# A macaron decoder layer on one core: paired units in a written order on VectorE and ScalarE, splits emitted a step ahead, gating weight tile by weight tile

## The chip, the cores and the metric

The kernel runs on one core of a Trainium2 chip. The metric is the device time of one execution in microseconds, the median of several runs. A core has a matrix engine (TensorE, PE in the profile), whose weight loads are shown as PEld, and VectorE (DVE), ScalarE (ACT), GpSimd (POOL) and SyncE (SP). Each executes its own list of instructions in order; semaphores tie the lists together. SP issues the DMA transfers here.

## The reference

One layer of a decoder, for 1024 tokens of width 1024 in float32:

```
x = x + 1/2 * SwiGLU_1(RMSNorm(x))            # d_ff = 2816
z = RMSNorm(x) @ w_in                          # [u | v | c_q | c_kv | k_rope | q_mem | gates A, B, C]
u, v = gelu(z_u), gelu(z_v)
y_a = u * (tril(W_s) @ layernorm(v) + b_s)     # spatial gating, chunks of 128 tokens, 8 groups of 64
y_b = latent attention(c_q, c_kv, k_rope)      # 8 heads, rotary, q and k normalized, causal
y_c = attention(q_mem, mem)                    # 4 heads, 256 memory tokens
x = x + (sum_i sigmoid(gate_i + b_gate) * (y_i @ W_branch_i)) @ w_out
x = x + 1/2 * SwiGLU_2(RMSNorm(x))
```

`SwiGLU(h)` is `(silu(h @ W_g) * (h @ W_u)) @ W_down`.

## The kernel before

**Precision.** Every float32 operand of a large matrix product is split: ACT rounds it to a high part (`split`, a cast or copy), DVE subtracts the high part from it for the low part. `mm3` then runs three matmuls: high by high, high by low, low by high. So each weight and each activation tile costs a pass of ACT, then one of DVE, before PE can use it: PE's second and third matmul of a group wait for the low parts.

**Seven products.** The feed-forward blocks and the gates are computed in blocks of two by two with seven products instead of eight (`Seven`). Activations have the operands b11, b12, b21, b22 and the sums t1 to t4; weights have a11, a12, a21, a22 and the sums s1 to s4. `OpNorm` makes the activation operands: `norm(half, p)` normalizes a tile, `put` splits it; t1, t2 and t4 come by one DVE addition or subtraction for each tile, in place, and t3 with b22 from the first half alone. `Seven.sums(f)` makes a unit's four weight sums on DVE, `Seven.weights(f, part)` splits the parts "a", "s", "t" and "l" of them. `product` is one call of 12 matmuls; a unit `f` of two output tiles takes seven such calls.

**The order of a block.** While the second half of the tokens is still being normalized, only t3 and b22 are ready. `units` therefore runs two units at once (f and g): first `s3*t3` and `s4*b22` for both; in between, `norm.sums(1)` (token sums of squares on PE, then an inverse square root on DVE) and `norm.turn(1)` (the scale turned by PE transposes into a PSUM bank); then, as b11, b21, t2, t1 and t4 appear, a11, a12, s2, s1 and a22 for both. After each output `emit` adds the pieces and applies the function (silu and product for a feed-forward block, sigmoid for a gate). `units` is called in three places: in `SwiGLU.start` for units 1 and 2 of FFN1, in `Gates.run` for gate units 0 and 1, and in `Kernel.run` for units 0 and 1 of FFN2. The remaining units go one by one through `unit` (`up`, `Gates.run`).

**Down.** `SwiGLU.down` is the second phase, again with seven products: seven loops, each over 11 tiles of the inner dimension in six steps of two (the last of one). A step fetches ahead, splits its weight tiles and its operand (`wide` gives the room: two tags of 5 buffers each), runs 24 matmuls into four banks, does the in-place sums that later loops need (`then`) and a few `acts` (accumulations of an earlier loop's banks into x, and the next norm's work). `next(aside)` advances a generator: `late_constants` loads 14 small constants and then makes rotary tables on DVE in pieces.

**Spatial gating.** `sgu` runs v and then u through `gelu_rows`, two tiles of 128 tokens at a time: `zrow` runs all eight weight tiles for one token tile, then for the next. v is normalized on DVE, split, and used as the operand of the gating products; u is multiplied by them.

**What sets the order.** Dependencies and semaphores come from the framework, and so does the order of each engine's list: a planner with a time model takes what is ready, the first emitted first. Inside `manual_schedule(engines=...)` the named engines keep the order of emission. In `start` these are PE, DVE, ACT and SP; in the other two calls of `units`, in `up` and the gates PE alone; in `down` PE and SP. Spatial gating is left to the planner.

In `units` the part after the first four calls reads, before:

```python
norm.b11(0)
if not early:
    w[f] |= self.weights(f, "a")
norm.b11(1)
for u in fs:
    ...
    self.product(a[u], w[u], "a11", "b11")
    p1[u] = k.row()
    nc.scalar.copy(p1[u], a[u])
    norm.b21(0 if u == f else 1)
```

Of the kernel before, what the change touches and what calls it, by code (L numbers as in the profile page):

```python
# [40 lines left out]
class Kernel:  # L41
# [506 lines left out]
    def gelu_rows(self, dst, h, i, w, pair):  # L548

        gelu = lambda d, x: self.nc.scalar.activation(d, x, ACT.Gelu)  # L550
        ps = self.mm() if pair else None
        for k in range(2):
            b = ps[:, k] if pair else self.bank()
            self.zrow(b, h, i + k, w)
            if not pair:
                gelu(dst[:, k], b)
        if pair:
            gelu(dst, ps)

    def sgu(self, h):  # L560
        nc, a, tc = self.nc, self.a, self.tc
        with tc.tile_pool(name="sgu", bufs=1) as p:
# [12 lines left out]
            for hf in range(2):  # L575
                vhi, vlo = (p.tile([P, 4, SGW], F32R, name=n, bufs=2) for n in ("v_hi", "v_lo"))
                vs.append((vhi, vlo))
                for i in range(0, 4, 2):
                    st = self.small.tile([P, 2, 6], F32, name="bn", tag="bn")
                    mv = self.small.tile([P, 2, 2], F32, name="mv", tag="mv")  # L580
                    v = self.raw().rearrange("p (k d) -> p k d", k=2)
                    self.gelu_rows(v, h, hf * 4 + i, w, i == 2)
                    for k in range(2):
                        nc.vector.bn_stats(st[:, k], v[:, k])
                        nc.vector.bn_aggr(mv[:, k], st[:, k])
                    r = self.rms(mv[:, :, 1], 2, 1)
                    for k in range(2):
                        nc.vector.scalar_tensor_tensor(
                            v[:, k], in0=v[:, k], scalar=mv[:, k, 0:1], in1=ln_g, op0=ALU.subtract, op1=ALU.mult)
                        nc.vector.scalar_tensor_tensor(  # L590
                            v[:, k], in0=v[:, k], scalar=r[:, k:k + 1], in1=ln_b, op0=ALU.mult, op1=ALU.add)
                    self.split(vhi[:, i:i + 2], vlo[:, i:i + 2], v)
            w = self.load(a["w_u"])
            yt = [self.split_pair() for _ in range(4)]
            for hf in range(2):
                u, v = p.tile([P, 4, SGW], F32, name="u"), vs[hf]
                for i in range(0, 4, 2):
                    self.gelu_rows(u[:, i:i + 2], h, hf * 4 + i, w, i == 0)
# [387 lines left out]
    def run(self):  # L986
# [12 lines left out]
        with tc.tile_pool(name="f1", bufs=1) as fp, self.banks("f1ps") as self.pm:  # L999
# [6 lines left out]
                lambda: nc.sync.dma_start(g_ffn1, a["ffn1_norm"]))  # L1006
            ffn.up(3)
# [7 lines left out]
            def sink(half, c):  # L1015
# [5 lines left out]
                [*first, *gates.first()], self.late_constants())  # L1021
# [4 lines left out]
        with tc.tile_pool(name="f2", bufs=1) as fp, self.banks("f2ps") as self.pm:  # L1026
# [9 lines left out]
            with tc.manual_schedule(engines={mybir.EngineType.PE}):  # L1036
                ffn.units((0, 1), early=True)
# [22 lines left out]
class OpNorm:  # L1060
# [22 lines left out]
    def norm(self, half, p, after=None):  # L1083


        t, s, v = self.t.t[half, p], self.s[half], self.k.nc.vector
        if self.scaled:
            i = v.tensor_tensor(t, t, s.unsqueeze(1).to_broadcast([P, 2, 512]), op=ALU.mult)
            if after is not None:
                self.k.after(i, after)  # L1090
            return t
        for k in range(2):
            c = 2 * p + k
            i = v.scalar_tensor_tensor(
                t[:, k], in0=t[:, k], scalar=self.gain()[:, c:c + 1], in1=s, op0=ALU.mult, op1=ALU.mult)
            if after is not None:
                self.k.after(i, after)
        return t

    def put(self, name, p, src, room=None):  # L1100
# [3 lines left out]
        self.mark = k.split(hi, lo, src)  # L1104
# [13 lines left out]
    def b11(self, p):  # L1118
        self.put("b11", p, self.norm(1, p))

    def b21(self, p):
        self.put("b21", p, self.norm(1, 2 + p, self.mark))

    def t2(self, p, room):

        t = self.t.t[1, p]
        self.k.nc.vector.tensor_tensor(t, self.t.t[0, p], t, op=ALU.add)
        self.put("t2", p, t, room)

    def t1(self, p, room):  # L1130
# [3 lines left out]
        self.put("t1", p, t, room)  # L1134

    def t4(self, p, room):
# [3 lines left out]
        self.put("t4", p, t, room)  # L1140


class Seven:
# [87 lines left out]
    def units(self, fs, w=(), late=0, turn=2, early=False, asides=()):  # L1231
# [11 lines left out]
        if early:  # L1243
            for f in fs:
                w[f] |= self.weights(f, "a")
# [15 lines left out]

        aside()
        norm.b11(0)
        if not early:
            w[f] |= self.weights(f, "a")
        norm.b11(1)
        for u in fs:
            a[u] = k.single()
            if u == g and not early:
                w[u] |= self.weights(u, "a")  # L1270
            self.product(a[u], w[u], "a11", "b11")
            p1[u] = k.row()
            nc.scalar.copy(p1[u], a[u])
            norm.b21(0 if u == f else 1)
# [3 lines left out]
        w[f] |= self.weights(f, "s")  # L1278
        for p in range(2):
            norm.t2(p, self.w4)  # L1280
        for u in fs:
            self.emit(u, 0, 1, None, a[u])
        w[g] |= self.weights(g, "s")
# [3 lines left out]
        for p in range(2):  # L1287
            norm.t1(p, self.w4)
# [4 lines left out]
        for p, u in enumerate(fs):  # L1293
            norm.t4(p, k.x4)
            w[u] |= self.weights(u, "l")
        for u in fs:
# [10 lines left out]
class Gates(Seven):  # L1307
# [26 lines left out]
    def run(self, x1d, r0):  # L1334
# [4 lines left out]
        with k.tc.manual_schedule(engines={mybir.EngineType.PE}):  # L1339
            self.units((0, 1), late=1, early=True)  # L1340
# [15 lines left out]
class SwiGLU(Seven):  # L1356
# [40 lines left out]
    def start(self, load_x, load_g):  # L1397
# [37 lines left out]
        with k.tc.manual_schedule(engines={E.PE, E.DVE, E.Activation, E.SP}):  # L1435
# [31 lines left out]
            self.units((1, 2), w, 0, 0, False, [lambda: (finish(0), keep(1), finish(1))])  # L1467
# [29 lines left out]
    def down(self, rows, load, sink, tasks=(), aside=iter(())):  # L1497
# [40 lines left out]

        def loop(n, acts=(), per=2):
# [3 lines left out]
            i, op, _, then = loops[n]  # L1543
            banks, held = [(k.single if n % 2 else k.bank)() for _ in range(4)], []
            for js in steps:
                m = len(js)
# [7 lines left out]
                t = ready.pop((n, js[0]))  # L1554
                wh, wl, th, tl = (k.wide(y).rearrange("p (a w) -> p a w", a=2) for y in ("whi", "wlo", "whi", "wlo"))
                for a, j in enumerate(js):
                    k.split(wh[:, a], wl[:, a], quad[j][i])
                k.split(th[:, :m], tl[:, :m], t)
                held += [(j, a, wh, wl, th, tl) for a, j in enumerate(js)]
# [47 lines left out]
        with k.tc.manual_schedule(engines={mybir.EngineType.PE, mybir.EngineType.SP}):  # L1607
            ahead()
            ahead()
            b = loop(0)  # L1610
# [87 lines left out]
```

## Time and profile before

| | |
|---|---|
| median of 3 runs | 2327.76 us |
| profiled execution | 2328.91 us |
| its span, first to last instruction | 2327.2 us |
| PE busy | 2225.2 us (96%) |
| DVE busy | 1560.0 us (67%) |
| ACT busy | 894.5 us (38%) |
| mean granted PE clock | 0.981 |
| HBM read, written | 201.80 MB, 82.31 MB |

The stages in the trace, in us from the start: FFN1's start to 56, its paired units to 116, its other units to 460, its down to 711; paired gate units to 769, other gates to 960; latent projections to 1068, spatial gating to 1180, memory and latent attention to 1560; the output projection to 1663; FFN2's paired units to 1720, its other units to 2088, its down to the end.

How to read the lines: a timeline row has its start and its length in us, engine, source line, operation, out<-in by the program's names and shapes, how often, and in brackets the idle time before it and what ended it. A window row has start and end, then the busy time (and instruction count) of PE, PEld, DVE, ACT and POOL, the granted PE clock as a share of full speed, the DMA engines' busy share and GB/s. A wait row has the engine and line that waited, what it waited for, the sum, the count and the longest. Line L125 is the cast of a split, L126 its subtraction. Names are those of the tiles: `h`, `w` and `x` hold operands and weights, `whi` and `wlo` the split weights, `bank`, `one` and `mm` are PSUM.

### The profile page before, as it was taken

The numbers are of one execution on the slowest core, as the hardware profiler recorded it, in microseconds if no ns is written. First come the engines' busy times: TensorE is split into PE (matmuls) and PEld (weight loads), VectorE is DVE, ScalarE is ACT, GpSimd is POOL, SyncE is SP. The second block draws the span as 40 slices with busy tenths as digits, with TensorE's granted clock in tenths as the row PEclk, the third lists the DMA queues.
The fourth block names the chain that finished last, engine by engine and source line by source line (L and its number), as shares of the span: only waits on it lengthen the run. The fifth ranks groups of instructions, "written<-read, shape, count | busy, mean of one in ns | idle before, by whom it ended". The sixth has DMA issues, their size and how long they took to land.

```text
span 2327.2 us, 27703 instructions
## 1 busy us (share of the span) xinstructions
PE 2225.2 (96%) x10286; PEld 1836.7 (79%) x10286; DVE 1560.0 (67%) x2481; ACT 894.5 (38%) x1493; POOL 260.0 (11%) x250
## 2 busy tenths in 40 slices
PE   8799999989998999999899999999989999999999
PEld 4488888877776788888778879978768888888777
DVE  6776666677787555458565758985776666668664
ACT  4322222233354333444243538843432222223333
POOL 0022212100000000003000031231012121210000
PEclk9899999999999999999999999999989999999999
DMA  3143333275341433215151371066023333328433
GB/s 127 34 141 104 107 108 102 96 276 186 109 145 46 136 116 129 98 55 163 55 168 62 117 264 48 28 237 220 37 92 107 104 106 111 104 99 309 151 119 103
DMA packets 117960, 285.94 MB, mean 123 GB/s; under 512 B 13888, under 2 KB 22208, under 8 KB 117696
## 3 DMA queue, kind: packets, MB, share of 16 engines
q1 hardware_dynamic: 117824, 284.16, 36.7%
q8 instruction: 81, 1.33, 0.2%
q14 instruction: 55, 0.45, 0.1%
HBM read 201.80 MB, written 82.31 MB: 122 GB/s over the span
## 4 chain that ended last, share of the span: by engine, by line
PE 41%; DVE 6%; DMA 4%; issue 2%; POOL 1%; ACT 1%; SPq 0%; POOLq 0%; DVEq 0%; ACTq 0%
PE bank L137 6%; PE bank L138 6%; PE bank L139 6%; PE one L138 5%; PE one L137 5%; PE one L139 5%; PE mm L137 2%; PE mm L138 2%; PE mm L139 1%; DVE wlo L126 1%; DMA t<-md 1%; PE bank L849 1%; PE bank L404 1%; PE bank L864 1%; PE bank L865 1%
## 5 line engine op out<-in xcount | busy, mean ns | idle before, releaser
L125 ACT CAST whi<-x 128x1024 fp32r<-128x1024 f32 (+1 forms) x193 | 181.9, 946 | 488.2 <-PE one L138 217.7
L126 DVE TENSOR_TENSOR wlo<-x,whi 128x1024 fp32r<-128x1024 f32 (+1 forms) x193 | 232.7, 1209 | 35.2 <-ACT whi L125 35.1
L137 PE MATMUL bank<-h,whi 128*128 128x512 f32 x644 | 251.8, 391 | 0.5 <-DVE t L931 0.3
L139 PE MATMUL bank<-h,wlo 128*128 128x512 f32 x644 | 251.1, 390 | 0.0
L138 PE MATMUL bank<-h,whi 128*128 128x512 f32 x644 | 251.0, 390 | 0.0
L1202 DVE TENSOR_TENSOR t<-t,one 128x512 f32<-128x512 f32 x139 | 95.6, 687 | 223.0 <-PE one L139 222.8
L125 ACT CAST whi<-w 128x1024 fp32r<-128x1024 f32 (+1 forms) x136 | 120.3, 899 | 313.6 <-PE one L138 137.6
L138 PE MATMUL one<-h,whi 128*128 128x512 f32 x476 | 190.5, 400 | 17.0 <-DVE h L126 17.0
L137 PE MATMUL one<-h,whi 128*128 128x512 f32 x476 | 190.5, 400 | 7.5 <-ACT whi L125 4.3
L126 DVE TENSOR_TENSOR wlo<-w,whi 128x1024 fp32r<-128x1024 f32 (+1 forms) x136 | 138.8, 1032 | 79.6 <-ACT whi L125 77.1
L139 PE MATMUL one<-h,wlo 128*128 128x512 f32 x476 | 189.1, 397 | 0.9 <-DVE wlo L126 0.9
L137 PE MATMUL one<-w,whi 128*128 128x512 f32 x392 | 153.6, 392 | 5.0 <-DVE t L1202 5.0
L139 PE MATMUL one<-w,wlo 128*128 128x512 f32 x392 | 153.3, 391 | 0.6 <-DVE wlo L126 0.6
L1477 POOL TENSOR_TENSOR raw<-raw 128x512 f32<-128x512 f32 x42 | 71.7, 1708 | 732.9 <-DVE raw L1377 732.8
L138 PE MATMUL one<-w,whi 128*128 128x512 f32 x392 | 153.3, 391 | 0.0
L138 PE MATMUL bank<-wlo,whi 128*128 128x512 f32 x352 | 140.6, 399 | 13.2 <-DVE wlo L126 13.2
L137 PEld LDWEIGHTS bank<-h,whi 128*128 128x128 f32 x644 | 121.3, 188 | 26.1 <-issue 0.7
L139 PEld LDWEIGHTS bank<-h,wlo 128*128 128x128 f32 x644 | 121.2, 188 | 25.3
L138 PEld LDWEIGHTS bank<-h,whi 128*128 128x128 f32 x644 | 121.2, 188 | 25.1 <-DVE h L126 0.2
L139 PE MATMUL bank<-whi,wlo 128*128 128x512 f32 x352 | 139.5, 396 | 0.0
L137 PE MATMUL bank<-whi 128*128 128x512 f32 x352 | 139.4, 396 | 0.0
L1202 DVE TENSOR_TENSOR raw<-t,one 128x512 f32<-128x512 f32 x109 | 74.8, 687 | 81.5 <-PE one L139 81.4
(369 smaller groups left out, 5067.0 us busy)
## 6 DMA issues: line engine op xcount, KB each, us to landing
x<-in_ffn_w_gu_dram SPq DMA_DIRECT2D x78, 512.0 KB, 5.3
w<-tdt SPq DMA_DIRECT2D x40, 512.0 KB, 4.4
tdb<-raw SPq DMA_DIRECT2D x66, 256.0 KB, 2.1
h<-in_ffn_w_down_dram SPq DMA_DIRECT2D x64, 256.0 KB, 6.0
w<-tdb SPq DMA_DIRECT2D x30, 512.0 KB, 4.7
gate<-raw SPq DMA_DIRECT2D x24, 512.0 KB, 2.9
t<-gate SPq DMA_DIRECT2D x48, 256.0 KB, 4.2
tdt<-w SPq DMA_DIRECT2D x44, 256.0 KB, 2.1
```

Source lines behind the costliest of these rows:

```text
L125: self.nc.scalar.copy(hi, src)
L126: return (eng or self.nc.vector).tensor_tensor(lo, src, hi.bitcast(F32), op=ALU.subtract)
L137: mmul(out, s[0], m[0], start=first, stop=False, **kw)
L138: mmul(out, s[0], m[1], start=False, stop=False, **kw)
L139: self.last = mmul(out, s[1], m[0], start=False, stop=last, **kw)
L404: nc.tensor.transpose(b[:m, k * P:(k + 1) * P], s, self.ident)
L849: nc.tensor.transpose(b[:, at:at + P], prs[t][:, kk * P:(kk + 1) * P], self.ident)
L864: nc.tensor.matmul(o, w, pt[0], start=n == 0, stop=False)
L865: nc.tensor.matmul(o, w, pt[1], start=False, stop=n == len(pts) - 1)
L1202: return self.nc.vector.tensor_tensor(out, x, y, op=ALU.add)
L1477: sub = lambda d, x, y: nc.gpsimd.tensor_tensor(d, x, y, op=ALU.subtract)
```

## The change

- `late_constants` is created before FFN1's `up`, and its 14 loads are emitted there; the table pieces stay in `down`.
- All three calls of `units` now keep the emission order on PE, DVE and ACT (`start` on SP too). `early` is gone; in the call of the gates `late` goes from 1 to 0, in those of gates and FFN2 `turn` from 2 to 1. Part "a" of f is split after the first product call where the sums follow there.
- In `units` the tiles are handled in pairs: both tiles of an operand are normalized or summed, then a weight part is split, then both tiles are split; the p1 copies come after both a11 calls, t2's additions and the s part of f.
- In `down` the splits of the next step (`prepare`) are emitted before the present step's matmuls, sums and acts.
- `gelu_rows` takes four token tiles at a time with the weight tiles as the outer loop, into the two PSUM pairs (first half) or the four banks (second half). v is kept in the buffer `u`, of which there is one, instead of the raw buffers.

```diff
-    def gelu_rows(self, dst, h, i, w, pair):
+    def gelu_rows(self, dst, h, w, pairs):
         gelu = lambda d, x: self.nc.scalar.activation(d, x, ACT.Gelu)
-        ps = self.mm() if pair else None
-        for k in range(2):
-            b = ps[:, k] if pair else self.bank()
-            self.zrow(b, h, i + k, w)
...
+        ps = [self.mm() for _ in range(2)] if pairs else [self.bank() for _ in range(4)]
+        for d in range(DT):
+            for i in range(4):
+                b = ps[i // 2][:, i % 2] if pairs else ps[i]
+                self.mm3(b, tuple(x[:, i * P:(i + 1) * P] for x in h[d]), w[d], d == 0, d == DT - 1)
+        for i, b in enumerate(ps):
+            gelu(dst[:, 2 * i:2 * i + 2] if pairs else dst[:, i], b)
...
+                rows = p.tile([P, 4, SGW], F32, name="u")
+                self.gelu_rows(rows, h[hf], w, hf == 0)
                 for i in range(0, 4, 2):
-                    v = self.raw().rearrange("p (k d) -> p k d", k=2)
-                    self.gelu_rows(v, h, hf * 4 + i, w, i == 2)
+                    v = rows[:, i:i + 2]
...
+            late = self.late_constants()
+            next(late)
             ffn.up(3)
...
-            with tc.manual_schedule(engines={mybir.EngineType.PE}):
-                ffn.units((0, 1), early=True)
+            with tc.manual_schedule(engines={E.PE, E.DVE, E.Activation}):
+                ffn.units((0, 1))
...
-    def units(self, fs, w=(), late=0, turn=2, early=False, asides=()):
+    def units(self, fs, w=(), late=0, turn=1, asides=()):
...
                 if n == late and 1 not in norm.r:
+                    w[f] |= self.weights(f, "a")
                     norm.sums(1)
...
-        norm.b11(0)
-        if not early:
+        b11 = [norm.norm(1, p) for p in range(2)]
+        norm.put("b11", 0, b11[0])
+        if "a11" not in w[f]:
             w[f] |= self.weights(f, "a")
-        norm.b11(1)
+        norm.put("b11", 1, b11[1])
+        w[g] |= self.weights(g, "a")
+        b21 = [norm.norm(1, 2 + p) for p in range(2)]
+        put("b21", b21)
         for u in fs:
             a[u] = k.single()
             self.product(a[u], w[u], "a11", "b11")
+        t2 = [norm.t2(p) for p in range(2)]
+        w[f] |= self.weights(f, "s")
+        for u in fs:
             p1[u] = k.row()
             nc.scalar.copy(p1[u], a[u])
-            norm.b21(0 if u == f else 1)
+        put("t2", t2, self.w4)
         for u in fs:
             self.product(a[u], w[u], "a12", "b21", False)
+        t1 = [norm.t1(p) for p in range(2)]
+        w[g] |= self.weights(g, "s")
+        put("t1", t1, self.w4)
         for u in fs:
             self.emit(u, 0, 1, None, a[u])
         for u in fs:
             z[u] = k.bank()
             self.product(z[u], w[u], "s2", "t2")
+        t4 = [norm.t4(p) for p in range(2)]
         for u in fs:
             v1[u] = k.row()
             self.add(v1[u], p1[u], z[u])
             self.product(z[u], w[u], "s1", "t1", False)
             w[u] |= self.weights(u, "l")
+        put("t4", t4, k.x4)
...
-            self.units((0, 1), late=1, early=True)
+        with k.tc.manual_schedule(engines={E.PE, E.DVE, E.Activation}):
+            self.units((0, 1))
...
+        def prepare(n, js):
+            ...
+            for a, j in enumerate(js):
+                k.split(wh[:, a], wl[:, a], quad[j][i])
+            k.split(th[:, :m], tl[:, :m], t)
+            split[n, js[0]] = [(j, a, wh, wl, th, tl) for a, j in enumerate(js)]
...
+                if s + 1 < len(steps):
+                    prepare(n, steps[s + 1])
+                elif n + 1 < len(loops):
+                    prepare(n + 1, steps[0])
+                held += split.pop((n, js[0]))
```

More of the change, by code (lines that the diff above doesn't have):

```diff
@@ L1020, in run @@
                 rows, lambda half, p: from_input(rows, half, p), sink,
-                [*first, *gates.first()], self.late_constants())
+                [*first, *gates.first()], late)
             gates.run(x1d, r0)
@@ L1081, in turn, with norm @@
         self.s[half] = k.norm_scale(self.r[half], late=k.last is not None)
[L1083 removed]
+    def norm(self, half, p):
         t, s, v = self.t.t[half, p], self.s[half], self.k.nc.vector
         if self.scaled:
[L1088 to L1090 removed]
+            v.tensor_tensor(t, t, s.unsqueeze(1).to_broadcast([P, 2, 512]), op=ALU.mult)
             return t
@@ L1537, in down @@
         loads = [(1, 2), (1, 3), (0, 2), (0, 3), (0, 0), (0, 1), (1, 0), (1, 1)]
+        split = {}
+        def prepare(n, js):
+            i, m = loops[n][0], len(js)
+            t = ready.pop((n, js[0]))
+            wh, wl, th, tl = (k.wide(y).rearrange("p (a w) -> p a w", a=2) for y in ("whi", "wlo", "whi", "wlo"))
+            for a, j in enumerate(js):
+                k.split(wh[:, a], wl[:, a], quad[j][i])
+            k.split(th[:, :m], tl[:, :m], t)
+            split[n, js[0]] = [(j, a, wh, wl, th, tl) for a, j in enumerate(js)]
         def loop(n, acts=(), per=2):
             acts = list(acts)
-            i, op, _, then = loops[n]
+            then = loops[n][3]
             banks, held = [(k.single if n % 2 else k.bank)() for _ in range(4)], []
-            for js in steps:
-                m = len(js)
+            for s, js in enumerate(steps):
                 ahead()
@@ L1609, in down @@
             ahead()
+            prepare(0, steps[0])
             b = loop(0)
```

57 lines of the change are left out of this document (16 added, 41 removed).

## The prediction

> **What bounds the kernel now.** I read the page first (busy shares), then the stretches that the diff touches as windows, then TensorE's (PE's) waits in each, and last the order of VectorE (DVE) and ScalarE (ACT) inside them.
>
> ```profile
> span 2327.2 us, 27703 instructions
> PE 2225.2 (96%) x10286; PEld 1836.7 (79%) x10286; DVE 1560.0 (67%) x2481; ACT 894.5 (38%) x1493; POOL 260.0 (11%) x250
> 140.00:160.00 20.00, 20.00 (x90) 16.57 (x89) 12.47 (x17) 5.50 (x7) 2.15 (x1) 1.00 0.42 128
> ```
>
> PE is busy for 96% of the span: it sets the time, and only its 102 us of idleness and the time that it spends at a lower clock can be won by a new order. In the quiet slice of the third row it starts 90 matmuls of 512 columns in 20 us: 0.222 us each, 2.7 for the 12 of one call of `product`.
>
> The next rows are the touched stretches in order: paired units of the first feed-forward block (FFN1), its second phase ("down"), paired gate units, spatial gating, paired units of FFN2, the unit behind them, FFN2's down. Columns: length, then PE, weight load, DVE, ACT and POOL busy, granted clock, DMA share, GB/s.
>
> ```profile
> 56.00:116.00 60.00, 43.46 (x144) 30.36 (x143) 42.73 (x44) 22.05 (x28) 4.28 (x3) 0.83 0.11 32
> 460.00:711.00 251.00, 235.89 (x1011) 191.82 (x1010) 190.33 (x308) 99.77 (x149) 4.88 (x4) 0.97 0.52 174
> 711.00:769.00 58.00, 45.36 (x184) 35.12 (x183) 47.08 (x65) 27.57 (x34) 0.00 (x0) 0.91 0.26 79
> 1068.00:1142.00 74.00, 66.97 (x295) 55.51 (x294) 57.07 (x138) 25.70 (x41) 12.55 (x12) 0.95 0.36 114
> 1663.00:1720.00 57.00, 48.35 (x199) 37.45 (x197) 41.42 (x60) 22.05 (x26) 0.05 (x1) 0.91 0.13 46
> 1720.00:1734.00 14.00, 10.67 (x39) 8.06 (x38) 12.57 (x13) 4.10 (x6) 7.82 (x4) 0.88 0.59 196
> 2088.00:2327.00 239.00, 229.69 (x993) 187.79 (x991) 156.17 (x218) 84.49 (x125) 4.61 (x3) 0.99 0.51 175
> ```
>
> Idle PE, length less the first busy column: 16.5, 15.1, 12.6, 7.0, 8.7, 3.3 and 9.3, together 72.5 us. Clock loss, length times (1 - clock): 10.2, 7.5, 5.2, 3.7, 5.1, 1.7 and 2.4, together 36. **About 108 us is all that the change can touch**, 4.7% of the span. The longest entries of PE's waits in these stretches (sum, count, longest) say who is late:
>
> ```profile
> PE bank L137 <- DVE t L1202: 5.1, 1, 5.1
> PE bank L138 <- DVE wlo L126: 8.4, 5, 3.0
> PE one L138 <- DVE wlo L126: 5.9, 3, 5.5
> PE one L138 <- DVE h L126: 7.7, 4, 4.1
> PE mm L137 <- ACT whi L125: 7.0, 1, 7.0
> PE one L138 <- DVE h L126: 7.3, 4, 3.8
> PE bank L138 <- DVE wlo L126: 4.8, 2, 2.8
> ```
>
> They are FFN1's units, down 1 (two rows), gates, spatial gating, FFN2's units and down 2. Mostly a split is late (ACT rounds to a high part, DVE subtracts for the low part), and seldom a transfer.
>
> **The change, part by part.** Sums are made against the profiled execution, 2328.9 us with a span of 2327.2. The median of the runs shown, 2327.8, is 1.1 lower; the gains are taken from it.
>
> *Paired units, FFN1.* Rows of DVE and ACT show the serial chain; the fifth gives the pace of narrow operations, the last the next unit's first matmul after both units' last ones:
>
> ```profile
> 56.84 1.22 DVE L1088 TENSOR_TENSOR x<-x,bank 128x1024 f32<-128x1024 f32 x1
> 59.16 1.23 DVE L126 TENSOR_TENSOR h<-x,h 128x1024 fp32r<-128x1024 f32 x1 [1.11 <-ACT h L125]
> 60.31 1.22 DVE L126 TENSOR_TENSOR wlo<-w,whi 128x1024 fp32r<-128x1024 f32 x1
> 77.06 1.23 DVE L126 TENSOR_TENSOR h<-x,h 128x1024 fp32r<-128x1024 f32 x1 [4.41 <-ACT h L125]
> 2232.93 1.28 DVE L1595 SCALAR_TENSOR_TENSOR w<-one,w 128x512 f32<-128x512 f32 x2
> 75.49 0.59 ACT L1273 COPY t<-one 128x512 f32<-128x512 f32 x1 [5.43 <-PE one L139]
> 115.82 0.39 PE L137 MATMUL one<-w,whi 128*128 128x512 f32 x1
> ```
>
> Norm, cast and subtraction follow one another; DVE waits 1.1 us for a cast, and 4.4 where the copy of p1, which waits for PE, stands ahead of b21's cast on ACT. The new order norms two tiles before it casts, and puts the p1 copies behind all b21 casts and a weight split. Back to back a 1024-wide operation takes DVE 1.15 us (59.16 to 60.31), a 512-wide one 0.60 (two in 1.28). Up to the last release of y I count 24 wide ones (10 for b11, b21 and the weights a, 5 for t2 with s of f, 5 for t1 with s of g, 4 for t4) and 10 narrow ones: 33.6 us, so from 56.84 to 90.4. Then follow the last product call (2.7) and the next unit's a11 (2.7), which before ran earlier than 115.82: 95.8, a gain of 20 at best. Against it stand about 3 for DVE's remaining waits (the first add behind its product call, a silu ahead of its gate), 3.5 for the next unit's sums and first split (four narrow, one wide), which before filled DVE's holes, and 2 for a slow clock. I take **12**; bounds 5 and 20.
>
> *Paired units, gates and FFN2.* Here DVE and ACT now get the written order too. The transposes of the second half's scale (`norm.turn`) come one product call earlier (2.7 us), and b21 is no longer overtaken on DVE by t2, t1 and t4, as it was at 741.7.
>
> ```profile
> 723.34 2.72 DVE L1094 SCALAR_TENSOR_TENSOR x<-x,c_mix_norm,bank 128x512 f32<-128x512 f32 x4 [2.56 <-PE bank L371]
> 741.70 1.22 DVE L126 TENSOR_TENSOR h<-x,h 128x1024 fp32r<-128x1024 f32 x1
> 768.29 0.39 PE L137 MATMUL one<-h,whi 128*128 128x512 f32 x1
> 1673.91 2.72 DVE L1094 SCALAR_TENSOR_TENSOR x<-x,c_ffn_norm,bank 128x512 f32<-128x512 f32 x4 [1.07 <-PE bank L371]
> 1719.74 0.39 PE L137 MATMUL one<-w,whi 128*128 128x512 f32 x1
> ```
>
> From the turn on DVE has 8 norms (0.66 each: four take 2.72), 19 wide and 9 narrow operations: 5.3 + 21.9 + 5.4 = 32.6 us; PE has 12 product calls, 32 us. Neither can be much shorter. Gates: 723.3 - 2.7 + 32.6 + 2.7 = 755.9 against 768.3, at best 12.4. Of it goes what the new place of the sums costs: PE reaches them after one product call and waits 1 to 2 us more for the last squares, with the second call queued behind; z of g waits about 1 for its s split. I take **9**; bounds 3 and 12. FFN2: 1671.2 + 32.6 + a gate (0.6) + 2.7 + the next unit's a11 (2.7) = 1709.8 against 1719.7, at best 10, and some of the 3.3 behind it. I take **7**; bounds 2 and 12.
>
> *Constants ahead of FFN1's up phase.* They leave down 1, where DVE stood behind the positions and then did the rotary tables first:
>
> ```profile
> 509.07 0.17 DVE L258 CAST pos<-pos_i 128x8 f32<-128x8 int32 x1 [2.95 <-DMA pos_i<-in_positions_dram]
> 511.87 1.22 DVE L126 TENSOR_TENSOR wlo<-w,whi 128x1024 fp32r<-128x1024 f32 x1
> 95.73 0.42 SPq L1484 DMA_DIRECT2D tdb<-raw  x1
> ```
>
> This is PE's wait of 5.5; with the slow clock behind it, about 7. On SP the loads wait for nothing, and SP there mostly waits for free buffers; without that cover they cost 14 issues of 0.42, 6 us, ahead of a unit's weights.
>
> *Splits a step ahead.* Emission is a priority for the planner here, not an order: it wins where sums stood in front, and nothing where DVE stands behind a transfer.
>
> ```profile
> 2163.48 1.29 DVE L1600 TENSOR_TENSOR x<-x,w 128x512 f32<-128x512 f32 x2 [5.18 <-DMA x<-x2d]
> 2234.13 1.89 DVE L1600 TENSOR_TENSOR x<-x,w 128x512 f32<-128x512 f32 x3
> 2235.93 1.22 DVE L126 TENSOR_TENSOR wlo<-w,whi 128x1024 fp32r<-128x1024 f32 x1
> 2237.20 0.50 PE L138 MATMUL bank<-wlo,whi 128*128 128x512 f32 x1 [1.93 <-DVE wlo L126]
> 2237.00:2242.00 5.00, 4.80 (x14) 3.81 (x15) 5.00 (x10) 0.00 (x0) 0.00 (x0) 0.66 0.56 166
> ```
>
> In down 2 the second wait can go (1.9, and 1.7 for 5 us at a clock of 0.66); of the first, 2.8, only the sums behind the transfer, 1.2. In down 1 five waits worth 8.4 are like the second; I take a third. With the constants **10** for down 1 (bounds 4 and 20), **3** for down 2 (0 and 7).
>
> The last two rows also show that a wait of 1.93 us is enough to bring the clock down. The Trainium skill (TensorE: Matmul & The Clock Gate, Part 1: The HAM clock gate) has it fall only after an idle window of about 3.4 us; that would leave short waits without a tail.
>
> *Gating k by k.* Four rows of tokens advance together, so a weight tile feeds 12 matmuls (2.7 us) before the next is wanted, instead of 3; and v no longer sits in the three raw buffers for which w_u's loads waited:
>
> ```profile
> 1118.29 7.91 SPq L91 DMA_DIRECT2D raw<-in_w_u_dram  x4
> ```
>
> The wait of 7.0 goes, and up to 3.7 of clock. In return one buffer `u` serves four passes, the first pass wants both PSUM pairs that the latent part still reads, and the second u pass takes all four banks that the gating products want: 1 to 3 us each. I take **4**; bounds -4 and 9.
>
> Sum: 12 + 9 + 7 + 10 + 3 + 4 = 45; 2327.8 - 45 = 2283, and with 1 us against me for the rest of the mixer, replanned from another start, **2284**. All lower bounds together give 2318, all upper 2248.
>
> **Rivals.** (a) *The order bites fully*: DVE's waits shrink to the counted work and the clock recovers. For it: DVE is under 85% busy in six of the seven stretches. A little over half of the way from my terms to their upper ends is 65, so 2263. (b) *The bound moves*: in the units DVE and PE need 32.6 and 32 us, and each wait of one delays the other; and the planner may depart from the emission where nothing is written by hand, so that the change isn't done there. Left are FFN1's chain at 9, the constants at 7 and gating at 4, with 2 from elsewhere: 2306. (c) *Full clock behind short waits*: my terms leave a wait of 2 to 3 us in each of the three calls, with 1.7 of clock each; without these 5 us it is 2279. The row at 2237 speaks against it. This is the rule of the Trainium skill named above. (d) *Slower: DVE parks behind early splits.* The cast of a split needs a buffer that PE frees at the end of a step; if its subtraction stands first on DVE, sums and accumulations queue behind it.
>
> ```profile
> 2234.86 1.05 ACT L125 CAST whi<-w 128x1024 fp32r<-128x1024 f32 x1 [3.38 <-PE bank L138]
> 480.00:500.00 20.00, 20.00 (x90) 16.53 (x89) 18.98 (x26) 7.84 (x12) 4.61 (x3) 1.00 0.86 311
> ```
>
> A step of 24 matmuls lasts 5.3 us; DVE has 4.0 of it on average in down 1 (190 of 251) and 5.0 in the busiest slice. Parked 2.6 us a step it loses 1.3: in 6 steps of 4 loops of both downs 62 us, less the 32 won elsewhere, 2358. It decides from 1.3 us a step. Against it: the casts wait for PE already now, and DVE fills that time.
>
> **How the numbers follow.** A measurement of this kernel tells about 2% from no change: faster means under 2281.2, slower over 2374.3. The forecast (2272 to 2299) has 0.50, of which 0.17 under 2281.2; (a) 0.17; (b) 0.20; (c) 0.08; (d) 0.05, of which 0.03 over 2374. Faster 0.17 + 0.17 + 0.08 = 0.42, slower 0.03, same 0.55; the forecast lies barely within 2%. The range 2264 to 2312 leaves out half of (a), the tail of (b) and (d).
>
> **What would show it.** In FFN1's units DVE over 85% busy and no copy of p1 ahead of a b21 cast; in gates and FFN2 no wait over 2 us at a12; in down no idleness of DVE for the positions; w_u loaded before 1110 and PE without a gap into u. I am wrong if waits over 3 us stand at z or s1 in the units, if DVE waits for ACT in every step of down, or if PE idles between gating and the memory branch.

## The result, and the profile after

The changed kernel takes 2271.7 us against 2326.8 for the kernel before on the same chip: ratio 0.9772, 95% interval 0.9753 to 0.9791. The prediction was 2284 with a range of 2264 to 2312, so the time lies in the range, 12 us under the forecast; the gain is 55 us where 44 were forecast, and it is just over the 2% that the prediction called a change ("same" had the larger chance there). One of the four runs of the kernel before took 11566 us and is not in the ratio; without it the median is 2325.9 and the gain 54 us.

The first lines of the page after:

```profile
span 2269.9 us, 27706 instructions
PE 2206.4 (97%) x10286; PEld 1829.1 (81%) x10286; DVE 1552.2 (68%) x2481; ACT 895.0 (39%) x1493; POOL 260.5 (11%) x250
```

PE, DVE and ACT run as many instructions as before; DVE is busy for 7.8 us less in total, ACT for 0.5 more. What changed is when. The touched stretches again, cut at the same matmuls as before (length, PE, weight load, DVE, ACT, POOL, granted clock, DMA share, GB/s):

```profile
57.32:100.47 43.15, 35.63 (x143) 27.36 (x142) 42.28 (x44) 22.00 (x28) 5.08 (x3) 0.96 0.14 44
444.60:686.50 241.90, 234.09 (x1010) 189.89 (x1009) 188.66 (x305) 100.10 (x149) 4.53 (x4) 0.99 0.53 180
686.50:735.90 49.40, 44.36 (x184) 35.16 (x183) 43.90 (x61) 25.54 (x31) 0.00 (x0) 0.93 0.23 68
1034.80:1100.90 66.10, 66.10 (x295) 54.91 (x295) 54.16 (x138) 24.59 (x40) 14.54 (x12) 1.00 0.41 128
1618.50:1667.70 49.20, 45.87 (x199) 37.01 (x198) 43.32 (x62) 24.13 (x29) 0.61 (x1) 0.97 0.16 54
1667.70:1677.30 9.60, 8.63 (x38) 6.83 (x37) 9.56 (x11) 1.79 (x3) 5.26 (x4) 1.00 0.56 169
2031.40:2269.90 238.50, 228.35 (x992) 186.50 (x990) 155.98 (x218) 84.70 (x125) 4.61 (x3) 0.99 0.51 175
```

PE's idle time in them (length less its busy column) is 34.8 us, where it was 72.5; the clock loss is 11.5, where it was 36. Spatial gating has no idle PE at all. FFN1's units have DVE busy for 42.3 of 43.2 us.

Both kernels have the same 10286 matmuls, so the n-th matmul of one trace can be set against the n-th of the other. The difference of their start times in the two profiled executions, read at the edges of the stages, gives each stage's gain (the terms are rounded):

```
stage                                  predicted   measured
start of FFN1, up to the units              0        -1.1
paired units, FFN1                         12        16.7
up phase of FFN1                            0         0.0
down 1: constants                           7         7.6
down 1: the rest                            3         1.5
paired units, gates                         9         8.7
spatial gating                              4         7.8
attention parts and projection             -1         3.5
paired units, FFN2, and the unit behind     7        12.2
down 2                                      3         0.6
sum                                        44        57.3
```

The two largest groups of PE's waits that are left in these stretches (line waited for, sum, count, longest):

```profile
PE bank L138 <- DVE wlo L126: 11.4, 8, 3.0
PE bank L137 <- DVE t L1194: 7.9, 3, 2.7
```

The first row is, but for 0.7 us, five of the waits in the two downs that were there before (1.4, 1.9, 3.0, then 2.5 and 1.9), nearly unchanged. The second is a wait of 2.6 to 2.7 us at s1 in each of the three calls of `units`: in the gates' and FFN2's it is new, in FFN1's it was 5.1 before.

### The profile page after: what moved, and what is told of

Read it like the earlier page. It is cut to its first block, busy times and chain, and to the rows that moved or that the text cites. A ratio compares the mean times of both kernels' runs of the same rounds, so it can differ in the third digit from the quotient of the medians.

```text
span 2269.9 us, 27706 instructions
## 1 busy us (share of the span) xinstructions
PE 2206.4 (97%) x10286; PEld 1829.1 (81%) x10286; DVE 1552.2 (68%) x2481; ACT 895.0 (39%) x1493; POOL 260.5 (11%) x250
## 4 chain that ended last, share of the span: by engine, by line
PE 80%; DVE 11%; DMA 4%; issue 3%; ACT 1%; SPq 1%; POOL 0%; DVEq 0%; POOLq 0%; ACTq 0%
PE one L138 12%; PE one L137 12%; PE one L139 12%; PE bank L137 11%; PE bank L138 11%; PE bank L139 11%; DVE wlo L126 3%; PE mm L137 2%; PE mm L138 2%; PE mm L139 2%; PE bank L849 1%; DVE x L1587 1%; PE bank L404 1%; DMA t<-md 1%; DMA w<-in_ffn_w_gu_dram 1%
## 5 line engine op out<-in xcount | busy, mean ns | idle before, releaser
L137 PE MATMUL one<-h,whi 128*128 128x512 f32 x476 | 187.4, 394 | 5.8 <-ACT t L1272 3.0
L138 PE MATMUL one<-h,whi 128*128 128x512 f32 x476 | 186.6, 392 | 0.8 <-DVE h L126 0.8
L138 PE MATMUL bank<-wlo,whi 128*128 128x512 f32 x352 | 140.0, 398 | 11.5 <-DVE wlo L126 11.4
```

The lines of the kernel that those rows point to most:

```text
L137: mmul(out, s[0], m[0], start=first, stop=False, **kw)
L138: mmul(out, s[0], m[1], start=False, stop=False, **kw)
```

## The experiments

Twelve kernels ran, each a small edit of the changed kernel. The table gives how much later (+) or earlier (-) than the changed kernel each is at the same matmul, at the edges of the stages. With it go the medians, and the ratio to the kernel before with its interval; differences under some 4 us can't be told from the ratios, and there the traces decide.

```
                   FFN1   units  down1  const. down1  gates  gating FFN2   unit   down2  end    median  ratio [95%]
                   units  end    start  over   end    end    end    units  behind start
kernel before      -1.1   15.6   15.8   23.4   24.6   33.3   41.1   44.6   56.8   56.8   57.3
e1  no ahead        0.4    0.4    2.0    2.0    0.9    0.8   -0.6    1.9    1.1    1.1    0.2   2272.3  0.9764 [0.9741, 0.9788]
e2  constants      -1.3   -1.3   -1.6    4.6    4.1    4.1    4.1    2.7    2.6    2.7    3.4   2279.7  0.9788 [0.9765, 0.9810]
e3  old gating      0.4    0.4    2.3    2.3    1.2    1.1    7.5    7.3    6.6    6.6    7.7   2280.5  0.9793 [0.9773, 0.9814]
e4  planned        -0.1   -0.1    0.4    0.3   -0.4    2.2    2.2    4.4    8.0    8.0    9.4   2282.0  0.9801 [0.9781, 0.9821]
e5  down by hand   -1.7   -1.6   -2.4   -2.9   -2.2    1.3    1.3    2.4    1.7    1.7   -8.0   2264.1  0.9715 [0.9696, 0.9734]
e6  same, no ahead -1.0   -0.8   -1.6   -2.1   10.3   12.7   12.6   11.2   10.5   10.5    0.8   2272.1  0.9748 [0.9725, 0.9771]
e7  t4 late         1.0    0.5    1.2    1.2    0.0   -0.1   -1.5    1.4    2.2    2.2    3.4   2270.9  0.9745 [0.9724, 0.9767]
e8  positions      -1.5   -1.6   -1.2   -1.3    0.4    0.3   -1.1    0.3   -0.5   -0.5    0.5   2272.0  0.9747 [0.9727, 0.9766]
e9  hand, no tasks -1.0   -1.8   -2.6   -3.2   -8.4   -8.5   -9.9   -5.8   -6.0   -6.0  -15.7   2255.4  0.9693 [0.9678, 0.9707]
e10 copies          0.0    4.0    5.2    5.2    4.1    4.0    4.2    6.7    6.0    6.0    5.4   2275.1  0.9779 [0.9764, 0.9793]
e11 one norm       -0.2    4.3    4.7    4.7    3.6    3.5    3.6    2.6    1.9    1.9    3.8   2277.7  0.9788 [0.9774, 0.9803]
e12 e9 and e8      -1.4   -1.4   -2.2   -2.8   -9.6   -9.7   -9.6   -8.9   -9.7   -9.7  -19.4   2251.8  0.9677 [0.9661, 0.9693]
```

One column warns of small sums: from the end of gating to FFN2's units, a stretch that e1, e2 and e5 to e12 don't touch, they shift by -1.4 to +4.1. This is no new order: PE's 2610, DVE's 691 and ACT's 560 instructions there stand in the same order in the changed kernel and in all of these. Part of it is the clock. The same wait of 2.59 us ahead of the same matmul (at 1157 us in the changed kernel) is in all fourteen traces; where the clock was 1.00 in the 5 us behind it, as in e2, the row gains 1.4 us there on the changed kernel, whose clock was 0.69. So one step of some 1.5 us in a row can be the clock alone. Each row is also one execution, which can lie off its kernel's median: e2's is 4.7 us under it, e7's 4.0 over it.

**e1: splits in their own step again.**

```diff
-                if s + 1 < len(steps):
-                    prepare(n, steps[s + 1])
-                elif n + 1 < len(loops):
-                    prepare(n + 1, steps[0])
+                prepare(n, js)
...
-            prepare(0, steps[0])
```

> The changed kernel, but in both second phases each step's splits are emitted in their own step again. Theory (on VectorE and ScalarE the planner's own order stands there, and emission is only a tie-break): 2270 to 2275 us against 2271.7, with TensorE's waits of 1.9 and 3.0 at a low part in place as in the changed kernel, and one more of 1.9 late in the first block's second phase. Rival (the early emission is worth what the prediction gave it, 3 us plus a third of 8.4): 2276 to 2279.

Measured 2272.3; the waits of 1.4, 1.9 and 3.0 stand where they stood, and the one of 1.9 late in down 1 does not come back (e8 shows why). VectorE runs the same instructions in the same order with and without the early emission, 305 in down 1 and 218 in down 2, and in down 2 the kernel before has this order too. So early emission is worth nothing here: the planner puts the split where it did anyway. What holds the split is seen in the changed kernel's order of time before the wait at 593 (start, length, engine, operation, idle before):

```profile
585.46 1.05 ACT L125 CAST whi<-w 128x1024 fp32r<-128x1024 f32 x1 [0.62 <-PE one L138]
...
586.59 1.89 DVE L1608 TENSOR_TENSOR x<-x,w 128x512 f32<-128x512 f32 x3
...
589.00 1.28 DVE L1603 SCALAR_TENSOR_TENSOR w<-one,w 128x512 f32<-128x512 f32 x2
590.20 1.89 DVE L1608 TENSOR_TENSOR x<-x,w 128x512 f32<-128x512 f32 x3
...
592.00 1.22 DVE L126 TENSOR_TENSOR wlo<-w,whi 128x1024 fp32r<-128x1024 f32 x1
593.27 0.50 PE L138 MATMUL bank<-wlo,whi 128*128 128x512 f32 x1 [1.94 <-DVE wlo L126]
```

The cast of 585.46 is done at 586.5; its subtraction (it is the only cast of that width still without one) runs at 592.0, with five sums of 0.6 us in a row directly ahead of it, accumulations of an earlier loop. Why the planner's time model puts them first isn't shown.

**e2: constants in down 1 again.**

```diff
-            late = self.late_constants()
-            next(late)
...
-                [*first, *gates.first()], late)
+                [*first, *gates.first()], self.late_constants())
```

> The changed kernel with the late constants loaded in the second phase again. Theory (they were the 5.5 us wait and its clock tail): the wait of TensorE for a low part behind the positions returns, 2278 to 2280 us against 2271.7, 7.2 us longer between 480 and 505. Rival (the early splits take the wait away as well, since the subtraction is emitted ahead of the tables): no more than 2 us, 2271 to 2274.

```profile
491.05 0.17 DVE L258 CAST pos<-pos_i 128x8 f32<-128x8 int32 x1 [2.94 <-DMA pos_i<-in_positions_dram]
495.16 0.79 PE L138 MATMUL one<-wlo,whi 128*128 128x512 f32 x1 [4.89 <-DVE wlo L126]
```

The wait is back (4.9 us), and between "down1 start" and "const. over" it loses 6.2 us, early splits or not: the theory holds. But at the start it is 1.3 us ahead of the changed kernel. In the changed kernel the planner has put the positions' cast, emitted for down 1, into the start of FFN1, ahead of a split:

```profile
26.35 0.15 DVE L790 TENSOR_SCALAR a_gq<-g_ev_q 96x1 f32<-96x1 f32 x1
29.00 0.17 DVE L258 CAST pos<-pos_i 128x8 f32<-128x8 int32 x1 [2.49 <-DMA pos_i<-in_positions_dram]
29.07 1.22 DVE L126 TENSOR_TENSOR h<-x,h 128x1024 fp32r<-128x1024 f32 x1
35.59 0.70 PE L1417 MATMUL one<-x,w 128*128 128x512 f32 x1 [2.73 <-ACT x L1410]
```

So the 1.1 us that the change loses at the start is this: DVE stands 2.5 us for the positions, and PE's wait at 36 us is 2.7 instead of 1.0; e8 tests it. In e5, e6, e9 and e12 the cast runs at 484 to 489 us, so their rows hold this gain as well.

**e3: gating as before.** `gelu_rows` and `sgu` are the old ones.

> The changed kernel with spatial gating row pair by row pair as before. Theory (the planner lays the attention parts out from where gating ends, so the 4.9 us won between gating and the second block's units belong to the gating edit): the 7.0 us wait for w_u returns and the later gain goes with it, 2281 to 2284 us. Rival (the later gain comes from another start of the planner's clock alone): only gating's own 6.4 us, 2277 to 2279, the attention parts as in the changed kernel.

```profile
PE mm L137 <- ACT whi L125: 6.8, 1, 6.8
```

Gating loses 7.9 us with this wait (from -0.3 just ahead of it to 7.5 behind), and the attention parts lose nothing more (7.5 to 7.3). The gating edit is worth its 7.8 us alone, and the 3.5 us in the attention parts are not its doing: the rival holds there. They lie within the spread named above and stay unexplained.

**e4: VectorE and ScalarE left to the planner in the gates' and FFN2's units.**

```diff
-        with k.tc.manual_schedule(engines={E.PE, E.DVE, E.Activation}):
+        with k.tc.manual_schedule(engines={E.PE}):
```

> The changed kernel with the planner free to order VectorE and ScalarE in the paired units of the gates and of the second block (the emission stays the new one). Theory (the written order on the two engines is what gains): the split of b21 is overtaken again, TensorE waits over 3 us there in both, 2283 to 2292 us. Rival (the new order of emission does it, the planner keeps it): 2270 to 2276.

It loses 2.5 us in the gates (-0.4 to 2.2) and 3.6 from FFN2's units on, all of it in the unit behind them; the 2.2 between lie within the spread named above. No wait over 3 us for b21 comes back; PE's longest for a split is 2.0 in each. The losses stand elsewhere: in the gates PE waits 3.8 us instead of 1.9 for the token sums, because on DVE three subtractions run between the two additions (L350) that these need, and in the unit behind FFN2's it waits 3.3 instead of 1.0 for a sum.

So neither theory holds whole: of the gates' 8.7 us about 6.2 remain without the written order on DVE and ACT, and 2.5 come from it; of FFN2's 12.2 it is 8.6 and 3.6. The part that remains is the new order of emission together with PE's own new order, which is written in e4 too; the two are not told apart here. Nor does the planner keep the emission: of e4's 59 DVE instructions in the gates' units only 37 stand in the changed kernel's order. But it keeps b21 ahead of the sums: its last subtraction, at 709.9, runs before t2's first addition, at 711.0, while in the kernel before it ran at 741.7, behind both additions of t2, both subtractions of t1 and one of t4.

**e5 and e6: both downs in written order on VectorE and ScalarE too, with and without early splits.**

```diff
-        with k.tc.manual_schedule(engines={mybir.EngineType.PE, mybir.EngineType.SP}):
+        with k.tc.manual_schedule(engines={
+                mybir.EngineType.PE, mybir.EngineType.SP, mybir.EngineType.DVE, mybir.EngineType.Activation}):
```

> The changed kernel, with VectorE and ScalarE in written order in both second phases too, so that a step's subtractions really stand in front of the preceding step's sums. Theory (the planner's order on VectorE is why the early splits brought nothing): the five waits of TensorE for a low part, 10.7 us by the profile, and some clock behind them go, 2256 to 2265 us against 2271.7. Rival (VectorE parks at the early subtractions until TensorE frees a buffer, as the prediction's slower case has it): 1.3 us a step, 2290 to 2360.

> As the run before, but with each step's splits emitted in their own step. Theory (in written order the early emission decides): the splits stand behind up to ten sums of the preceding step, TensorE waits 1 to 3 us in most of the 42 steps of both phases, 2290 to 2340 us. Rival (the written order alone does it, wherever the splits stand): 2256 to 2270, as with early splits.

e5: 2264.1. All five waits for a low part in the downs are gone, 9.7 us in down 2 alone (1.7 to -8.0). DVE stands 60.2 us at the casts there, 50.9 in the changed kernel, but holds up nothing by it. In down 1 one new wait eats the gain. First its rows in e5, then PE's waits at the same place in e6:

```profile
654.41 1.40 DVE L1094 SCALAR_TENSOR_TENSOR x<-x,c_mix_norm,bank 128x512 f32<-128x512 f32 x2
...
655.96 0.77 PE L137 MATMUL bank<-whi 128*128 128x512 f32 x1 [10.88 <-DVE x L1094]
```

```profile
PE bank L137 <- ACT whi L125: 8.4, 2, 6.7
PE one L138 <- DVE wlo L126: 4.4, 1, 4.4
```

In the last two loops the next norm stands between the steps. In written order its chain (norm, cast, subtraction) alternates with the splits, the last norm has read the scale only at 655.8, and the scale sits in a PSUM bank that the last loop's products want. e6, without early splits, gains as much in down 2 (10.5 to 0.8) and in down 1 up to the matmul at 600 us (7.9, e5 8.2), and loses 19.0 us behind it, where e5 loses 7.6. Its rival was right outside those last loops: the written order does it, early splits or not. Early splits are worth something, 11 us, only where the order is written and long tasks stand between the steps; e9 shows that the planner does better there.

**e9 and e12: written order in the downs except in down 1's last two loops; e12 with the positions' cast held as well.**

> As the run with both second phases by hand, but in the first block's last two loops of the second phase (those with the norm's and the gates' tasks between the steps) VectorE and ScalarE are the planner's again. Theory (TensorE's wait of 10.9 us at 656, behind norms that stand in front of a split, is the price of the written order in those loops alone): it goes, at most the 3.0 us of the changed kernel's wait comes back, 2253 to 2258 us against 2264.1. Rival (the planner's tasks are late anyway once the loops before them are shorter): 2262 to 2266.

> The first kernel of this call, with the positions' cast held until the first block's units are done as well. Theory (in the run that held the cast alone, its 1.7 us at the start were given back by the planner's new order of the second phase, a wait of 1.9 at 660; written order there leaves it no such choice): 1 to 2 us under the first kernel of this call, 2251 to 2257. Rival (something else gives it back, in the first block's units as before): the same time within 0.7 us.

```profile
PE bank L138 <- DVE wlo L126: 4.8, 2, 3.0
```

That is e9's row of the waits in down 1, the 3.0 of the changed kernel and a 1.9: 2255.4 us, as expected. e12 takes 2251.8, the fastest here, but not for the reason given: in e9 the positions' cast could not leave the written order anyway (PE's wait at the start is 1.0 in both). e12's lead over e9 is 1.2 us at the end of down 1, where the 1.9 is absent, and the rest in the untouched stretch behind gating. All four runs of e12 lie under all four of e9, so the 3.6 us between the medians are more than the spread of either; what makes them isn't shown.

**e7, e8, e10, e11: VectorE's order in the units, and the positions.** e7 writes t4 behind the two sums v1 (and the splits of the parts l behind t4); e8 holds the cast until the units are done:

```diff
-        t4 = [norm.t4(p) for p in range(2)]
         for u in fs:
             v1[u] = k.row()
...
+        t4 = [norm.t4(p) for p in range(2)]
```

```diff
-        v.tensor_copy(pos, pos_i)
+        self.after(v.tensor_copy(pos, pos_i), self.hold)
```

> The changed kernel, with the two subtractions of t4 written behind both sums v1 in the paired units. Theory (TensorE's wait of 2.6 us at s1, which stands in all three calls, is VectorE's order alone): the three waits go and half of them does not come back, 2264 to 2269 us. Rival (VectorE is the bound of the paired units, it works without a hole up to the last sums): the wait moves to a22 or to the next unit, 2270 to 2273.

> The changed kernel, with the cast of the positions held on VectorE until the first block's paired units are done; the loads stay. Theory (the planner put this cast into the first block's start, where VectorE waits 2.5 us for its load and the first splits come late): TensorE's wait at 36 us falls from 2.7 to 1.0, the span by 1.5, 2269 to 2271 us. Rival (the fourteen small loads themselves delay the start): no change, 2271 to 2273.

> The changed kernel; in the first block's paired units alone, the copies of p1 stand again on ScalarE ahead of the two casts of b21. Theory (VectorE has no hole from 58 to 90 us there, so each delay of it reaches the end): the second cast waits for the second product a11, VectorE 3 us for it, and the units end 2 to 4 us later, 2274 to 2276. Rival (the end is set by the products and the slow clock, with some slack on VectorE): less than 1 us, 2271 to 2273.

> The changed kernel; in the first block's paired units alone, b21's and b11's tiles are normed, cast and subtracted one after the other again. Theory: VectorE waits 1.1 us for each of three or four casts, the units end 3 to 4.5 us later, 2274 to 2276. Rival (weight splits fill those waits): less than 1 us, 2271 to 2273.

e7: the waits at s1 go, and others of 1.4 to 2.1 us stand behind the last sums instead; 2270.9, no difference that can be told. The rival holds. e8: the start gains its 1.5 us, and a wait of 1.9 is back at 660, the one that the kernel before had at 684; again no difference that can be told. That wait is not a matter of order: DVE's 305 and ACT's 148 instructions of down 1 stand in e8 as in the changed kernel. It goes by the clock behind the wait of 2.95 us shortly before. First the changed kernel, then e8:

```profile
653.98 0.50 PE L138 MATMUL bank<-wlo,whi 128*128 128x512 f32 x1 [2.95 <-DVE wlo L126]
653.98:658.98 5.00, 5.00 (x15) 3.98 (x16) 5.00 (x8) 1.90 (x3) 0.00 (x0) 0.66 0.30 105
661.63 0.50 PE L138 MATMUL bank<-wlo,whi 128*128 128x512 f32 x1 [0.30 <-DVE wlo L126]
```

```profile
652.70 0.50 PE L138 MATMUL bank<-wlo,whi 128*128 128x512 f32 x1 [2.95 <-DVE wlo L126]
652.70:657.70 5.00, 5.00 (x22) 4.14 (x23) 5.00 (x8) 1.90 (x3) 0.00 (x0) 1.00 0.31 105
660.36 0.50 PE L138 MATMUL bank<-wlo,whi 128*128 128x512 f32 x1 [1.91 <-DVE wlo L126]
```

At the full clock PE comes to the next late split sooner, and waits there. Of the twelve traces with the 2.95 the kernel before, e8 and e9 had a clock of 1.00 behind it, and these three have the 1.9; the other nine had 0.66, and 0.3.

e10 has the p1 copies ahead of b21's casts again in FFN1's units, e11 norms one tile at a time there; they lose 4.0 and 4.5 us in the units alone. e11's median is 2 us over what was expected; its traced execution is its fastest, 2275.3, and doesn't show where. VectorE's waits in FFN1's units for ACT's casts, first e10, then e11, then the kernel before (the changed kernel has none there):

```profile
DVE h L126 <- ACT h L125: 4.1, 2, 2.3
```

```profile
DVE h L126 <- ACT h L125: 4.5, 4, 1.2
```

```profile
DVE h L126 <- ACT h L125: 9.7, 4, 4.4
DVE w L126 <- ACT w L125: 4.5, 4, 1.2
DVE x L126 <- ACT x L125: 2.2, 2, 1.1
DVE wlo L126 <- ACT whi L125: 0.7, 1, 0.7
```

What VectorE waits there, the end of the units loses, one for one: 4.1 and 4.0, 4.5 and 4.5, and 17.1 (the four rows) against the 16.7 that the change won.

## Why the prediction was right, and where it was off

**FFN1's units: mechanism right, the gain sized too low.** The count of 24 wide and 10 narrow operations up to the last release of y was right, and so was 33.6 us for them. But they do not run to the end by themselves:

```profile
58.09 2.35 DVE L1090 TENSOR_TENSOR x<-x,bank 128x1024 f32<-128x1024 f32 x2
...
88.42 1.21 DVE L126 TENSOR_TENSOR wlo<-x,whi 128x1024 fp32r<-128x1024 f32 x1
...
92.37 0.69 DVE L1375 TENSOR_TENSOR raw<-raw,t 128x512 f32<-128x512 f32 x1 [0.70 <-ACT t L1379]
...
93.58 1.46 DVE L1168 TENSOR_TENSOR x<-x,x 128x512 f32<-128x512 f32 x1
94.97 1.77 DVE L1173 TENSOR_TENSOR x<-x 128x512 f32<-128x512 f32 x1
96.67 0.67 DVE L1194 TENSOR_TENSOR raw<-t,bank 128x512 f32<-128x512 f32 x1
...
97.39 0.50 PE L137 MATMUL bank<-x,whi 128*128 128x512 f32 x1 [0.55 <-DVE raw L1194]
```

The last release is the row at 96.67, which PE's last call waits for; from 58.09 to its end are 39.3 us. Among the counted operations stand the next unit's first split (88.42) and two of its sums (93.58 and 94.97), 4.2 us, and DVE waits 0.7 for a silu. So of the 8.5 us that I set against the 20, the 3.5 for the next unit came, as 4.2, and the 3 for DVE's waits did not. Against them the next unit's a11, 2.7, was not left for the end: it ran at 91.2. In all 3.3 us were lost. The row that gives the term directly was the sum of VectorE's waits for ScalarE, 17.1 us.

**Gates: 8.7 against 9. FFN2's units: 12.2 against 7**, just over the upper bound of 12: 8.8 in the units, and 3.4 in the unit behind, where the prediction spoke of "some of the 3.3" and gave no figure. It took the two kinds of edit as one; e4 shows that the new emission with PE's new order does the larger part and the written order on DVE and ACT the smaller.

**Constants: 7.6 against 7, but the cost was looked for on the wrong engine.** The prediction feared SP's 14 issues; it was DVE, because an instruction left to the planner is not tied to where it is emitted. The cost is 1.1 us.

**Splits a step ahead: the step that failed.** "In down 2 the second wait can go" and "a third" of 8.4 in down 1: e1 shows no gain in either. The prediction named the reason, a priority and not an order, and still priced a gain. The 1.5 us of down 1's rest are the wait of 1.9 that goes by the clock (absent in e1, back in e8), and so no work of the change. In rival (d) DVE parks and delays PE; where the order is really written (e5) DVE does wait more for the casts, and PE loses nothing by it.

**Gating: 7.8 against 4.** The wait and the clock went, as said; the 1 to 3 us each that I charged for the single `u` and for the banks did not appear: PE is busy for all of the 66.1 us. But the stretch is only 7.9 us shorter, not 10.7, the 7.0 of the wait and the 3.7 of the clock. The clock loss was sized too high, here and in the 108 us: length times (1 - clock) counts a low clock while PE idles, too (in the kernel before it was 0.69 from 1117 to 1122 us, where PE did nothing). In the seven stretches PE's idle time fell by 37.7 us and its busy time by 17.4, together the 55.1 by which they are shorter; the clock loss by the formula fell by 24.5.

**The sum.** The time is within the range, but its parts are not the forecast ones. The 3.5 us of the attention parts are traced to no edit, and the 1.5 of down 1 are the clock's; without these five the time would have been some 7 us from the forecast, not 12. That the gates came out at the forecast 9 is in part luck: of the two prices set against them PE's wait for the last squares came (1.9 us, 1.1 before), the one at z did not, and the wait of 2.6 at s1 stands instead.

**Rivals.** The time lies between the forecast and (a), a little nearer to (a), and for (a)'s reason in the units. (b) did not happen where the order was written by hand, and did in the downs. (c) is answered below.

## What to carry to other kernels

In a stretch that one engine's serial work bounds, as VectorE's does in FFN1's units, the sum of that engine's waits for its partner was the size of the gain from reordering; subtract only what a row shows. It does not size a stretch in which the engine is merely given the wrong work first: in the gates VectorE waited only 1.8 us for ScalarE before, and the gain was 8.7.

Moving emission under a planner is not yet a change of order: it did nothing in the downs, and held most of the gain in the gates. Compare the order that was run, and to be sure of it write the order on the engine that is late, leaving out the loops in which long tasks stand between the steps. Instructions that the planner may move can land far ahead of their place, so an early load should go with a hold on its first reader.

## What the runs showed of the hardware

A short wait of TensorE does not always bring the clock down. The same wait of 1.94 us ahead of the same matmul, in the changed kernel and in e4, with the 5 us behind it (columns as above):

```profile
2179.84 0.50 PE L138 MATMUL bank<-wlo,whi 128*128 128x512 f32 x1 [1.94 <-DVE wlo L126]
2179.84:2184.84 5.00, 5.00 (x15) 3.93 (x16) 5.00 (x9) 0.00 (x0) 0.00 (x0) 0.66 0.52 156
```

```profile
2190.34 0.50 PE L138 MATMUL bank<-wlo,whi 128*128 128x512 f32 x1 [1.94 <-DVE wlo L126]
2190.34:2195.34 5.00, 5.00 (x22) 4.16 (x23) 5.00 (x9) 0.00 (x0) 0.00 (x0) 1.00 0.48 152
```

Over the fourteen traces, of 58 waits of 1.85 to 1.95 us 38 were followed by a clock below 0.95 in the next 5 us. After the first 45 us so were 50 of 65 waits of 2.5 to 3.1 us, and all 19 over 3.1; the longest without a drop is 3.08 us, in e2. What decides it in the shorter ones isn't shown. So a tail like the one that the prediction gave to waits of about 2 us holds about two times in three. Rival (c) did not occur: behind the three waits at s1, for which it expected the full clock, the changed kernel's clock was 0.66 each time. The Trainium skill (TensorE: Matmul & The Clock Gate, Part 1: The HAM clock gate) calls the window of some 3.4 us free-running; that agrees with a drop that comes at the same matmul in one run and not in another, while its rule of a whole idle window doesn't fit drops behind waits of 1.9 us.
